# A Strassen-Winograd quad that accumulates two of its seven products in banks of two others

## The chip, the cores and the metric

One core of one Trainium2 chip runs the kernel. The metric is the device time of one execution in microseconds (us); lower is better. TensorE multiplies into PSUM, which has 8 banks of 128x512 fp32 values in this program's use. VectorE (DVE), ScalarE (ACT) and GpSimd (POOL) work on the rest, SP issues the loads.

## The reference

A decoder block on x (1024 tokens by 1024), fp32 in and out:

```
h  = rms_norm(x)
u  = h @ w_in            # recurrent x and gate, q, k, v, two branch gates
y1 = rg_lru(conv4(xr)) * gelu(gr)                  # 16 blocks of 64 channels
y2 = dilated_window_attention(rope(q), rope(k), v) # 3 groups of 4 heads, 128 wide
x1 = x + rms_norm((y1 @ w_lp * sigmoid(gl) + y2 @ w_ap * sigmoid(ga)) @ w_out)
out = x1 + rms_norm((silu(h2 @ w_fg) * (h2 @ w_fu)) @ w_dn),   h2 = rms_norm(x1)
```

D_FF is 2816. The norms have gains. The result is compared at fp32 accuracy, so each fp32 product is made of three matmuls in a faster format: each operand is split into a high part and a rest.

## The kernel before

`split` (L98, L99) makes the two parts of an operand: a copy on ScalarE (names that end in hi or h) and a subtraction on VectorE (lo or l). `mm3` (L133 to L135) issues the three matmuls high by high, rest by high, high by rest for each 128 rows of the contraction.

Most projections are done as 50 objects `Quad`: 28 in phase 1 (four for gr, four for xr, twelve for q and k, eight for the gates gl and ga) and 22 for the FFN (w_fg and w_fu in turn). A quad computes four 128x512 outputs, written (n, u), from two raw 128x1024 weights r0 and r1, with Winograd's form of Strassen's algorithm: seven products P1 to P7 of twelve 128x512 matmuls each, so 84 matmuls a quad. POOL makes the sums of weights sa and sb from r0 and r1 (L267 to L270). Three weight units of a quad go through `split`: r0 for P1 and P2, sa for P6 and P7, sb for P5 and P3; the upper half of r1, for P4, has buffers of its own (w4h, w4l). The pool of the units, tags whi and wlo, has three buffers for each, which go round in the order r0, sa, sb, next r0. The raw weights (tag wraw) have two.

The products run in the order P1, P2, P6, P5, P3, P7, P4, each in its own bank. ScalarE copies P1 out as p1 (L294, `keep`). VectorE adds:

```
out(0,0) = P2 + p1      u2 = P6 + p1      w = P5 + u2      out(0,1) = P3 + w
out(1,1) = P7 + w       v  = P7 + u2      out(1,0) = P4 + v
```

`plus` (L309) makes u2, w and v; the outputs go through `out`, which is L720 in phase 1 (with a function on ScalarE, L722, where there is one, then a DMA), `gate` (L1232 and Silu, L1233) and `up` (L1238, and a product on POOL, L1239) in the FFN. `run_quads` is the loop; after each product `tick` counts, and at fixed counts it emits pieces of other work between the products: the LRU with its convolution (L768 to L800, products `pgt` with operands xch and xcl), and the rotation of q and k (`rotate`, L811 to L816, operands rq, rcs, rsn by DMA).

Phase 1 starts with a stage of its own (0 to 50 us): x arrives, transposed parts are split (`put`, L425 and L426), the squares of the rows give the rates of the norm (`rates`, L439 to L451: square root on ScalarE, five small steps on VectorE, the diagonal dg, and a matmul prb that spreads them), `normed` (L457) scales x, `v0_mm` (L463) makes the first v and `v0_out` (L479) copies it out. The first two quads of phase 1 (PRE1) get their first products ahead of the loop, while the rotary tables are made. At the FFN the list ORDER sets the work ahead of the loop: t is the transposition of a token tile, p the loading of a quad's r0, h a quad's P1 and P2, x the sums of operand columns (splits L562, L563 and differences on POOL, L566).

The order of the instructions on each engine is set by a scheduler from the order in which the program emits them; `tc.issue_after` puts an instruction behind a named one. Loads keep the order of the program on SP.

## Time and profile before

| | |
|---|---|
| median of 3 runs | 1753.15 us (1753.12 to 1754.28) |
| the profiled execution | 1749.78 us |
| its span, first to last instruction | 1748.0 us |
| busy: TensorE, VectorE, ScalarE, GpSimd | 96%, 64%, 42%, 40% |
| mean granted TensorE clock | 0.978 |
| chain that ended last: TensorE, VectorE, DMA | 77%, 8%, 5% |

The profile is of one execution. Busy time is time with an instruction at work; the granted clock is 1.00 at 2.4 GHz and 0.50 at 1.2 GHz. The waits name, for each idle stretch of an engine, the instruction that ended it. Times within the span count from its first instruction.

### The profile page before, as it was taken

The numbers are of one execution on the slowest core, as the hardware profiler recorded it, in microseconds if no ns is written. First come the engines' busy times: TensorE is split into PE (matmuls) and PEld (weight loads), VectorE is DVE, ScalarE is ACT, GpSimd is POOL, SyncE is SP. The second block draws the span as 40 slices with busy tenths as digits, with TensorE's granted clock in tenths as the row PEclk, the third lists the DMA queues.
The fourth block names the chain that finished last, engine by engine and source line by source line (L and its number), as shares of the span: only waits on it lengthen the run. The fifth ranks groups of instructions, "written<-read, shape, count | busy, mean of one in ns | idle before, by whom it ended". The sixth has DMA issues, their size and how long they took to land.

```text
span 1748.0 us, 21093 instructions
## 1 busy us (share of the span) xinstructions
PE 1676.7 (96%) x7748; PEld 1376.2 (79%) x7748; DVE 1113.9 (64%) x1585; ACT 727.5 (42%) x1130; POOL 698.0 (40%) x650
## 2 busy tenths in 40 slices
PE   8999999999999988989999999799999999999996
PEld 6897888787877876878888887678888888788885
DVE  6966676778788665563433577755545555649658
ACT  6423367554555522464451345422222222344343
POOL 2003354554445434214334204576556566400103
PEclk9899999999999999999999999899999999999998
DMA  8233433333333455584618742133222222475353
GB/s 319 73 133 113 148 133 124 135 137 129 127 133 133 139 166 179 197 330 155 229 50 304 269 162 84 49 115 133 102 103 91 103 91 103 150 261 198 109 186 121
DMA packets 95919, 262.70 MB, mean 150 GB/s; under 512 B 13768, under 2 KB 22120, under 8 KB 94408
## 3 DMA queue, kind: packets, MB, share of 16 engines
q1 hardware_dynamic: 70352, 182.49, 30.7%
q0 software_dynamic: 20352, 76.21, 11.5%
q10 hardware_dynamic: 5112, 2.66, 0.5%
q8 instruction: 61, 1.00, 0.2%
q14 instruction: 42, 0.34, 0.1%
HBM read 180.86 MB, written 80.35 MB: 149 GB/s over the span
## 4 chain that ended last, share of the span: by engine, by line
PE 77%; DVE 8%; DMA 5%; issue 4%; POOL 3%; ACT 2%; SPq 1%; ACTq 0%; DVEq 0%; POOLq 0%
PE pq L135 14%; PE pq L134 14%; PE pq L133 14%; PE pd L1334 4%; PE pd L1335 4%; PE pd L1333 4%; DMA rsn<-rtd 3%; PE py L135 2%; PE py L134 2%; PE py L133 2%; PE pv L463 2%; PE po L1017 2%; PE pv L133 1%; PE pv L135 1%; PE pv L134 1%
## 5 line engine op out<-in xcount | busy, mean ns | idle before, releaser
L135 PE MATMUL pq<-hth,wlo 128*128 128x512 f32 x448 | 179.7, 401 | 9.8 <-DVE wlo L99 9.8
L133 PE MATMUL pq<-hth,whi 128*128 128x512 f32 x448 | 179.6, 401 | 2.8 <-ACT whi L98 2.8
L134 PE MATMUL pq<-htl,whi 128*128 128x512 f32 x448 | 180.7, 403 | 0.0
L267 POOL TENSOR_TENSOR sb<-wraw 128x512 f32<-128x512 f32 x50 | 71.6, 1432 | 173.1 <-DMA wraw<-in_w_fg 92.3
L98 ACT ACTIVATE whi<-sa 128x1024 fp32r<-128x1024 f32 x50 | 53.0, 1059 | 201.5 <-PE pq L134 126.8
L1334 PE MATMUL pd<-fbl,fah 128*128 128x512 f32 x304 | 119.7, 394 | 4.5 <-DVE fbl L99 4.5
L1335 PE MATMUL pd<-fbh,fal 128*128 128x512 f32 x304 | 119.7, 394 | 0.0
L1333 PE MATMUL pd<-fbh,fah 128*128 128x512 f32 x304 | 119.3, 393 | 0.0
L98 ACT ACTIVATE whi<-wraw 128x1024 fp32r<-128x1024 f32 x67 | 70.7, 1055 | 98.2 <-PE pq L134 25.8
L135 PEld LDWEIGHTS pq<-hth,wlo 128*128 128x128 f32 x448 | 86.0, 192 | 32.1 <-DVE wlo L99 11.6
L99 DVE TENSOR_TENSOR wlo<-wraw,whi 128x1024 fp32r<-128x1024 f32 x67 | 91.6, 1367 | 26.4 <-ACT whi L98 23.7
L309 DVE TENSOR_TENSOR uw<-pq,uw 128x512 f32<-128x512 f32 x100 | 68.3, 683 | 60.2 <-PE pq L135 59.5
L133 PEld LDWEIGHTS pq<-hth,whi 128*128 128x128 f32 x448 | 86.0, 192 | 24.7 <-ACT whi L98 3.2
L134 PEld LDWEIGHTS pq<-htl,whi 128*128 128x128 f32 x448 | 85.9, 192 | 20.5
L1407 POOL TENSOR_TENSOR y<-y,gpf 128x512 f32<-128x512 f32 x16 | 25.2, 1602 | 186.9 <-ACT fah L98 109.5
L99 DVE TENSOR_TENSOR wlo<-sa,whi 128x1024 fp32r<-128x1024 f32 x50 | 70.1, 1401 | 28.6 <-ACT whi L98 28.6
L1239 POOL TENSOR_TENSOR fo<-fo,ut 128x512 f32<-128x512 f32 x44 | 60.6, 1381 | 67.1 <-DVE ut L1238 67.1
L720 DVE TENSOR_TENSOR fb<-pq,uw 128x512 f32<-128x512 f32 x84 | 67.8, 807 | 29.4 <-PE pq L135 29.0
L99 DVE TENSOR_TENSOR fal<-ar,fah 128x1024 fp32r<-128x1024 f32 (+1 forms) x41 | 50.5, 1231 | 51.5 <-ACT fah L98 51.4
L98 ACT ACTIVATE fah<-ar 128x1024 fp32r<-128x1024 f32 (+1 forms) x41 | 40.8, 995 | 100.9 <-PE pd L1334 79.5
L133 PE MATMUL pq<-t1h,whi 128*128 128x512 f32 x200 | 79.6, 398 | 0.9 <-ACT whi L98 0.9
L134 PE MATMUL pq<-t1l,whi 128*128 128x512 f32 x200 | 79.4, 397 | 0.0
(542 smaller groups left out, 4948.0 us busy)
## 6 DMA issues: line engine op xcount, KB each, us to landing
ar<-fd SPq DMA_DIRECT2D x35, 512.0 KB
qkd<-fb POOLq DMA_DIRECT2D x24, 512.0 KB, 3.6
qk<-qkd SPq DMA_DIRECT2D x24, 512.0 KB
wraw<-in_w_fg SPq DMA_DIRECT2D x24, 512.0 KB
wraw<-in_w_fu SPq DMA_DIRECT2D x24, 512.0 KB
fd<-fo POOLq DMA_DIRECT2D x11, 1024.0 KB, 4.3
wd<-in_w_dn SPq DMA_DIRECT2D x21, 512.0 KB
fd<-fs POOLq DMA_DIRECT2D x11, 768.0 KB, 5.6
```

What stands on the lines that cost most here:

```text
L98: A.activation(hi, src, AF.Copy)
L99: (le or V).tensor_sub(lo, src, f(hi))
L133: T.matmul(o, lh, rh, start=(first and i == 0), stop=False)
L134: T.matmul(o, lh, rl, start=False, stop=False)
L135: T.matmul(o, ll, rh, start=False, stop=(last and i == n - 1))
L267: G.tensor_add(sb[:, lo_], r1[:, lo_], r1[:, hi_])
L309: V.tensor_add(y, bank, x)
L720: V.tensor_add(o, half_in(bank, g), half_in(add, g))
L1239: G.tensor_mul(g, g, ut)
L1333: T.matmul(o, ah[:, ts], bh, start=(i == 0), stop=False)
L1334: T.matmul(o, ah[:, ts], bl, start=False, stop=False)
L1335: T.matmul(o, al[:, ts], bh, start=False, stop=(i == NP - 1))
```

## The change

Each quad now runs P1, P6, P5, P7, P2, P4, P3 in five banks. P2 is accumulated onto P1 in P1's bank (`head2`), after ScalarE has copied p1 out, so that the bank then holds out(0,0) itself; P3 is accumulated onto P5, after ScalarE has copied that out as c1. The additions are

```
u2 = P6 + p1    v = P7 + u2    out(1,1) = c1 + v    out(1,0) = P4 + v    out(0,1) = (P5 + P3) + u2
```

Out(0,0) needs none: in phase 1 and in `gate` ScalarE reads the bank, with the function in the same instruction; in `up` VectorE multiplies the bank with the gate in place. In the ORDER of the FFN, a is P1 with its copy and b is P2. The buffers uw go from three to two, c1 has one. In the start stage some instructions are put behind others: the second `rates` chain, `v0_out`, and the splits `put`.

```diff
-ORDER = [(s[0], int(s[1])) for s in "t6 h1 p2 p3 x5 h0 t7 x6 x4 h2 x7 h3".split()]
+ORDER = [(s[0], int(s[1])) for s in "t6 a1 p2 p3 x5 a0 b1 t7 x6 x4 a2 b0 x7 a3 b2 b3".split()]
...
-        def mm(self, p):
-            bank = ps("pq")
+        def mm(self, p, bank=None):
+
+            first = bank is None
+            bank = bank or ps("pq")
             wh, wl = self.w[p]
             xh, xl = Quad.X[self.NAMES[p]]
             mm3(bank, [(wh[:, 128 * k:128 * k + 128], wl[:, 128 * k:128 * k + 128],
-                        xh[:, k, :], xl[:, k, :]) for k in range(4)])
+                        xh[:, k, :], xl[:, k, :]) for k in range(4)], first, skip_group_check=not first)
...
-        def start_mm(self):
-            self.b = self.mm("P1"), self.mm("P2")
+        def head1(self):
+            self.b = self.mm("P1")
 
         def keep(self):
             self.p1 = Quad.pool.tile([128, 512], F32, name="p1", bufs=Quad.P1B)
-            A.activation(self.p1, self.b[0], AF.Copy)
-
-        def head(self):
-            self.start_mm()
-            self.keep()
+            A.activation(self.p1, self.b, AF.Copy)
+
+        def head2(self):
+            self.mm("P2", self.b)
+            self.whole = True
 
         def first(self):
-            if self.start:
-                self.start()
-            self.out(0, 0, self.b[1], self.p1)
-
-        def body(self):
-
-            def plus(bank, x):
-                y = Quad.up.tile([128, 512], F32, name="uw", bufs=3)
-                V.tensor_add(y, bank, x)
-                return y
-
-            u2 = plus(self.mm("P6"), self.p1)
-            yield
-            w = plus(self.mm("P5"), u2)
-            yield
-            self.out(0, 1, self.mm("P3"), w)
-            yield
-            bank = self.mm("P7")
-            self.out(1, 1, bank, w)
-            v = plus(bank, u2)
-            yield
-            self.out(1, 0, self.mm("P4"), v)
-            if self.done:
-                self.done()
-            yield
+            self.out(0, 0, self.b, None)
 
     def run_quads(quads, pre, tick=None):
+        def plus(bank, x):
+            y = Quad.up.tile([128, 512], F32, name="uw", bufs=2)
+            V.tensor_add(y, bank, x)
+            return y
+
+        step = tick or (lambda: None)
         quads[0].prep()
-        for j in range(pre):
-            quads[j].first()
+        for q in quads[:pre]:
+            if q.whole:
+                q.start()
+                q.first()
         for j, q in enumerate(quads):
             if j + 1 < len(quads):
                 quads[j + 1].prep()
-            for _ in q.body():
-                if tick:
-                    tick()
-            if pre <= j + 1 < len(quads):
-                quads[j + 1].head()
-                if tick:
-                    tick()
-                quads[j + 1].first()
-                if tick:
-                    tick()
+            if j >= pre:
+                q.head1()
+                q.keep()
+                step()
+            if not q.whole:
+                q.start()
+            u2 = plus(q.mm("P6"), q.p1)
+            step()
+            c = q.mm("P5")
+            c1 = Quad.up.tile([128, 512], F32, name="c1", bufs=1)
+            A.activation(c1, c, AF.Copy)
+            step()
+            v = plus(q.mm("P7"), u2)
+            q.out(1, 1, c1, v)
+            step()
+            if not q.whole:
+                q.head2()
+                q.first()
+                step()
+            q.out(1, 0, q.mm("P4"), v)
+            step()
+            q.out(0, 1, q.mm("P3", c), u2)
+            if q.done:
+                q.done()
+            step()
...
-            V.tensor_scalar(dg[:, t], ident, e[:, t:t + 1], None, op0=OP.mult)
+            last_dve[0] = V.tensor_scalar(dg[:, t], ident, e[:, t:t + 1], None, op0=OP.mult)
...
-            put(0, j)
-            w0_split(j)
+            with tc.issue_after(last_dve[0].ins):
+                put(0, j)
+                w0_split(j)
...
-    v0_out(bk0, 0, r0)
+    with tc.issue_after(last_act[0].ins):
+        v0_out(bk0, 0, r0)
     with tc.issue_after(last_rb[0].ins):
         v0_mm(bk1, 1, 1)
     v0_mm(bk1, 1, 2)
     v0_mm(bk1, 1, 3)
-    for j in range(4):
-        normed(1, j, rb)
-    for j in range(4):
-        put(0, j)
+    with tc.issue_after(last_dve[0].ins):
+        for j in range(4):
+            normed(1, j, rb)
+        for j in range(4):
+            put(0, j)
...
-            V.tensor_add(o, half_in(bank, g), half_in(add, g))
-            if fn is not None:
-                A.activation(o, o, fn)
+            if add is None:
+                A.activation(o, half_in(bank, g), fn or AF.Copy)
+            else:
+                V.tensor_add(o, half_in(bank, g), half_in(add, g))
+                if fn is not None:
+                    A.activation(o, o, fn)
...
-        q1[j].start_mm()
+        q1[j].head1()
...
-            V.tensor_add(g, bank, add)
-            A.activation(g, g, AF.Silu)
+            if add is not None:
+                V.tensor_add(g, bank, add)
+            A.activation(g, bank if add is None else g, AF.Silu)
 
         def up(n, u, bank, add):
             g = FO[i][:, 2 * n + u, :]
-            ut = op.tile([128, 512], F32, name="ut", bufs=UT)
-            V.tensor_add(ut, bank, add)
-            G.tensor_mul(g, g, ut)
+            if add is None:
+                V.tensor_mul(g, bank, g)
+            else:
+                ut = op.tile([128, 512], F32, name="ut", bufs=UT)
+                V.tensor_add(ut, bank, add)
+                G.tensor_mul(g, g, ut)
...
+    def head(j):
+        quads[j].head1()
+        quads[j].keep()
+
     for step, j in ORDER:
-        {"p": pre, "h": lambda q: quads[q].head(), "t": e_turn, "x": x_cols}[step](j)
+        {"p": pre, "a": head, "b": lambda q: quads[q].head2(), "t": e_turn, "x": x_cols}[step](j)
```

What moves, in three places.

VectorE in the start stage, from the end of the first four `normed` blocks on. Before:

```order
L426 TENSOR_TENSOR htl_122<-x,hth_120 128x2x512
L441 RECIPROCAL rr_379<-rs_377 128x4
L426 TENSOR_TENSOR htl_122<-x,hth_120 128x2x512
L443 SCALAR_TENSOR_TENSOR re_381<-ss_172,rr_379 128x4
L426 TENSOR_TENSOR htl_123<-x,hth_121 128x2x512
L444 SCALAR_TENSOR_TENSOR re_381<-re_381,rr_379 128x4
L426 TENSOR_TENSOR htl_123<-x,hth_121 128x2x512
L445 SCALAR_TENSOR_TENSOR re_381<-re_381,rr_379 128x4
L99 TENSOR_TENSOR wlo<-wraw,whi 128x1024
L446 TENSOR_SCALAR rr_379<-re_381 128x4
L449 TENSOR_SCALAR dg<-cst,re_381 128x128 x4
L457 SCALAR_TENSOR_TENSOR x<-x,gneg,prb 128x512 x8
```

Now:

```order
L459 SCALAR_TENSOR_TENSOR x<-x,gneg,prb 128x512 x6
L443 RECIPROCAL rr_379<-rs_377 128x4
L445 SCALAR_TENSOR_TENSOR re_381<-ss_172,rr_379 128x4
L446 SCALAR_TENSOR_TENSOR re_381<-re_381,rr_379 128x4
L447 SCALAR_TENSOR_TENSOR re_381<-re_381,rr_379 128x4
L448 TENSOR_SCALAR rr_379<-re_381 128x4
L451 TENSOR_SCALAR dg<-cst,re_381 128x128 x4
L428 TENSOR_TENSOR htl_122<-x,hth_120 128x2x512
L459 SCALAR_TENSOR_TENSOR x<-x,gneg,prb 128x512 x8
L428 TENSOR_TENSOR htl_122<-x,hth_120 128x2x512
L428 TENSOR_TENSOR htl_123<-x,hth_121 128x2x512 x2
L99 TENSOR_TENSOR wlo<-wraw,whi 128x1024 x2
```

The steps of the second `rates` chain (rr, re, dg), which alternated with splits (htl, wlo), follow each other; the splits come behind the chain.

TensorE at the hand-over, from the last matmul of the heads on. Tiles pq are the banks: 1463 is P2 of quad 1, 1546 and 1580 are P6 and P5 of quad 0. Before:

```order
L135 MATMUL pq_1463<-hth1_121,wlo_1447 128x512
L133 MATMUL pq_1546<-hth0_120,whi_1505 128x512 [waits PE_49,Activation_49]
L134 MATMUL pq_1546<-htl0_122,whi_1505 128x512
L133 MATMUL pq_1580<-t1h1_499,whi_1509 128x512 [waits PE_49,Activation_49]
L134 MATMUL pq_1580<-t1l1_500,whi_1509 128x512
L135 MATMUL pq_1546<-hth0_120,wlo_1506 128x512 [waits DVE_49]
```

Now, with 1418 and 1437 as P1 of quads 0 and 1, and 1515 as P6 of quad 0:

```order
L135 MATMUL pq_1437<-hth0_120,wlo_1434 128x512
L133 MATMUL pq_1418<-hth1_121,whi_1414 128x512 [waits Activation_49]
L134 MATMUL pq_1418<-htl1_123,whi_1414 128x512
L135 MATMUL pq_1418<-hth1_121,wlo_1415 128x512
L133 MATMUL pq_1418<-hth1_121,whi_1414 128x512
L133 MATMUL pq_1515<-hth0_120,whi_1479 128x512 [waits PE_49,Activation_49]
L134 MATMUL pq_1515<-htl0_122,whi_1479 128x512
L134 MATMUL pq_1418<-htl1_123,whi_1414 128x512
L135 MATMUL pq_1515<-hth0_120,wlo_1480 128x512 [waits DVE_49]
```

The P2 of quad 0 (L133 with hth1 into 1418) follows the two P1 and waits for ScalarE. Four of its matmuls stand ahead of P6, a fifth behind the first two of P6; the other seven, and the twelve of quad 1's P2, come after the matmul that waits for wlo.

VectorE in the FFN, one quad of the gate with the splits of the next quad's weights among its additions. Before (uw is u2, w and v, fo the outputs):

```order
L1232 TENSOR_TENSOR fo_10508<-pq_10493,p1_10506 128x512
L99 TENSOR_TENSOR wlo_10522<-wraw_10511,whi_10521 128x1024
L309 TENSOR_TENSOR uw_10550<-pq_10537,p1_10506 128x512
L309 TENSOR_TENSOR uw_10565<-pq_10552,uw_10550 128x512
L1232 TENSOR_TENSOR fo_10508<-pq_10567,uw_10565 128x512
L99 TENSOR_TENSOR wlo_10526<-sa_10515,whi_10525 128x1024
L1232 TENSOR_TENSOR fo_10508<-pq_10582,uw_10565 128x512
L309 TENSOR_TENSOR uw_10597<-pq_10582,uw_10550 128x512
L99 TENSOR_TENSOR wlo_10530<-sb_10516,whi_10529 128x1024
L99 TENSOR_TENSOR w4l_10534<-wraw_10513,w4h_10533 128x512
L1232 TENSOR_TENSOR fo_10508<-pq_10599,uw_10597 128x512
```

Now:

```order
L309 TENSOR_TENSOR uw_9890<-pq_9877,p1_9874 128x512
L309 TENSOR_TENSOR uw_9920<-pq_9907,uw_9890 128x512
L1241 TENSOR_TENSOR fo_9876<-c1_9905,uw_9920 128x512
L99 TENSOR_TENSOR wlo_9846<-wraw_9835,whi_9845 128x1024
L99 TENSOR_TENSOR wlo_9850<-sa_9839,whi_9849 128x1024
L99 TENSOR_TENSOR w4l_9858<-wraw_9837,w4h_9857 128x512
L1241 TENSOR_TENSOR fo_9876<-pq_9937,uw_9920 128x512
L1241 TENSOR_TENSOR fo_9876<-pq_9892,uw_9890 128x512
L99 TENSOR_TENSOR wlo_9854<-sb_9840,whi_9853 128x1024
```

Of the seven additions five are left. The split of r0 stood before u2 and comes after out(1,1); the split of sb comes last, after the addition of P3.

## Rows read from the trace of the kernel before

**Rows 1.** Stretches of the span (from:to in us). Columns: length, then busy us and instructions (x) of TensorE's matmuls, of its weight loads, of VectorE, ScalarE and GpSimd, then the granted TensorE clock (1.00 is full speed), the busy share of the DMA engines, GB/s.

```profile
0.00:50.00 50.00, 38.45 (x144) 28.64 (x145) 32.87 (x54) 26.25 (x37) 12.34 (x14) 0.92 0.80 300
...
150.00:165.00 15.00, 11.31 (x42) 8.44 (x41) 6.17 (x8) 6.68 (x9) 9.01 (x10) 0.90 0.33 106
...
350.00:400.00 50.00, 50.00 (x217) 40.38 (x216) 39.02 (x48) 27.52 (x33) 27.22 (x23) 1.00 0.39 140
...
420.00:450.00 30.00, 26.38 (x102) 20.60 (x101) 23.97 (x24) 12.13 (x15) 9.39 (x9) 0.89 0.27 97
...
500.00:550.00 50.00, 49.73 (x212) 39.54 (x212) 45.18 (x50) 25.54 (x32) 22.09 (x20) 1.00 0.34 119
...
650.00:700.00 50.00, 45.06 (x174) 35.44 (x174) 29.09 (x39) 13.43 (x20) 21.22 (x21) 0.90 0.54 182
...
1100.00:1120.00 20.00, 11.19 (x32) 7.61 (x31) 17.33 (x19) 7.96 (x11) 11.21 (x9) 0.66 0.15 52
...
1130.00:1500.00 370.00, 368.81 (x1610) 301.78 (x1609) 200.09 (x215) 104.66 (x134) 233.76 (x178) 1.00 0.29 107
```

**Rows 2.** TensorE's waits over the whole span, the four longest kinds and one more that the prediction counts: the waiting line <- the engine and line waited for: us in total, times, longest.

```profile
PE pq L135 <- DVE wlo L99: 11.4, 6, 4.7
PE pq L133 <- ACT whi L98: 10.0, 4, 5.7
PE prb L451 <- DVE dg L449: 7.0, 1, 7.0
PE pgt L133 <- ACT xch L98: 3.9, 3, 2.2
PE pgt L134 <- DVE xcl L99: 3.3, 5, 1.4
```

**Rows 3.** Groups of instructions over the whole span: VectorE's additions from a bank in the Quads. Behind the bar: busy us, mean ns of one, then idle time before and what ended it.

```profile
L309 DVE TENSOR_TENSOR uw<-pq,uw 128x512 f32<-128x512 f32 x100 | 68.3, 683 | 60.2 <-PE pq L135 59.5
L720 DVE TENSOR_TENSOR fb<-pq,uw 128x512 f32<-128x512 f32 x84 | 67.8, 807 | 29.4 <-PE pq L135 29.0
```

**Rows 4.** Timeline of TensorE in the first 50 us: start, us, line, output <- inputs; in brackets the idle time before and its releaser.

```profile
12.18 2.29 PE L463 MATMUL pv<-wlo,hth 128*128 128x512 f32 x8 [2.09 <-DVE wlo L420]
46.74 2.04 PE L451 MATMUL prb<-dg,ones 128*128 128x512 f32 x2 [6.95 <-DVE dg L449]
```

**Rows 5.** Timeline of VectorE, the chain of L441 to L449 in its two runs: the first and the last row of each.

```profile
22.10 0.17 DVE L441 RECIPROCAL rr<-rs 128x4 f32<-128x4 f32 x1
...
22.97 0.87 DVE L449 TENSOR_SCALAR dg<-cst,re 128x128 f32<-128x128 f32 x4
...
40.84 0.17 DVE L441 RECIPROCAL rr<-rs 128x4 f32<-128x4 f32 x1
...
45.73 0.86 DVE L449 TENSOR_SCALAR dg<-cst,re 128x128 f32<-128x128 f32 x4
```

**Rows 6.** Timeline of ScalarE before the second run of that chain: a split of an operand and the square root (L439).

```profile
38.60 1.06 ACT L425 ACTIVATE hth<-x 128x1024 fp32r<-128x1024 f32 x1
39.55 0.29 ACT L439 ACTIVATE rs<-ss,epsc 128x4 f32<-128x4 f32 x1
```

**Rows 7.** Timeline of TensorE at the hand-over to the Quads: the 25th and the 48th matmul of P1 and P2, and the first ones after them.

```profile
151.65 0.40 PE L133 MATMUL pq<-hth,whi 128*128 128x512 f32 x1
...
157.02 0.40 PE L135 MATMUL pq<-hth,wlo 128*128 128x512 f32 x1
...
160.16 0.50 PE L133 MATMUL pq<-hth,whi 128*128 128x512 f32 x1 [2.75 <-ACT whi L98]
...
161.84 0.77 PE L133 MATMUL pq<-t1h,whi 128*128 128x512 f32 x1 [0.94 <-ACT whi L98]
```

**Rows 8.** Timeline of ScalarE there: the two p1 copies (one row, x2) and the split of the first sa.

```profile
156.61 1.09 ACT L294 ACTIVATE p<-pq 128x512 f32<-128x512 f32 x2 [5.10 <-DMA rtd<-rot]
159.05 1.06 ACT L98 ACTIVATE whi<-sa 128x1024 fp32r<-128x1024 f32 x1 [0.84 <-POOL sa L268]
```

**Rows 9.** The three multiply-adds (L770) of the convolution of one channel block, for two blocks: min/median/max ns, first and last start us.

```profile
L770 DVE SCALAR_TENSOR_TENSOR xc<-xr__3408,vec,xc x3: 744/745/751, 402.3 to 404.3; 128x512 f32<-128x512 f32 x3
L770 DVE SCALAR_TENSOR_TENSOR xc<-xr__3603,vec,xc x3: 752/3208/4284, 425.6 to 433.2; 128x512 f32<-128x512 f32 x3
```

**Rows 10.** Timeline of VectorE in the rotary zone: the last split of a quad's weights (w4l), the second rotation's first product (rm), the split of sa behind it, the next w4l.

```profile
651.93 0.68 DVE L99 TENSOR_TENSOR w4l<-wraw,w4h 128x512 fp32r<-128x512 f32 x1
...
670.41 0.69 DVE L811 TENSOR_TENSOR rm<-rq,rsn 128x512 f32<-128x512 f32 x1 [2.00 <-DMA rsn<-rtd]
...
673.29 1.21 DVE L99 TENSOR_TENSOR wlo<-sa,whi 128x1024 fp32r<-128x1024 f32 x1
...
677.96 0.68 DVE L99 TENSOR_TENSOR w4l<-wraw,w4h 128x512 fp32r<-128x512 f32 x1
```

**Rows 11.** Timeline of VectorE before the FFN's Quads: the same split of one operand part, at two times.

```profile
1087.00 0.68 DVE L563 TENSOR_TENSOR t1l<-h2f,t1h 128x512 fp32r<-128x512 f32 x1
...
1094.67 1.79 DVE L563 TENSOR_TENSOR t1l<-h2f,t1h 128x512 fp32r<-128x512 f32 x1
```

**Rows 12.** Timeline of ScalarE in a quad of the FFN's steady part: the split of sb and the p1 copy.

```profile
1283.02 1.06 ACT L98 ACTIVATE whi<-sb 128x1024 fp32r<-128x1024 f32 x1 [1.64 <-PE pq L134]
...
1288.72 0.60 ACT L294 ACTIVATE p<-pq 128x512 f32<-128x512 f32 x1 [4.64 <-PE pq L135]
```

**Rows 13.** Timeline of VectorE there: the second half of that split of sb.

```profile
1284.74 2.00 DVE L99 TENSOR_TENSOR wlo<-sb,whi 128x1024 fp32r<-128x1024 f32 x1
```

More of the change, by code (lines that the diff above doesn't have):

```diff
@@ L128, in h_tiles, with mm3 @@
         return ts, [ts[k // 4][:, k % 4, :] for k in range(KT)]
-    def mm3(o, terms, first=True, last=True):
+    def mm3(o, terms, first=True, last=True, **kw):
         n = len(terms)
         for i, (lh, ll, rh, rl) in enumerate(terms):
-            T.matmul(o, lh, rh, start=(first and i == 0), stop=False)
-            T.matmul(o, lh, rl, start=False, stop=False)
-            T.matmul(o, ll, rh, start=False, stop=(last and i == n - 1))
+            T.matmul(o, lh, rh, start=(first and i == 0), stop=False, **kw)
+            T.matmul(o, lh, rl, start=False, stop=False, **kw)
+            T.matmul(o, ll, rh, start=False, stop=(last and i == n - 1), **kw)
     def gain_bc(ap, name, eng=None, mk=None):
@@ L237, in block @@
         w = None
+        whole = False
         def __init__(self, src, out, start=None, done=None):
-            self.src, self.out, self.start, self.done = src, out, start, done
+            self.src, self.out, self.start, self.done = src, out, start or (lambda: None), done
         def unit(self, src, names):
```

## Prediction

> **What bounds the kernel now.** I read the stretches of the span first, then TensorE's waits, then the rows around each wait. In the stretches [rows 1] the reader is to see that TensorE is full for most of the span: 217 matmuls in the 50 us from 350, 1610 in the 370 us of the FFN's gate and up. That is 0.230 us for each, at a granted clock of 1.00, and no engine behind it can make it shorter. What the change can win or lose lies in the stretches that are not full: the start (38.45 of 50 us busy, clock 0.92), the hand-over to the quads at 150 to 165 (42 matmuls where 65 fit), 420 to 450 (clock 0.89), 650 to 700 (174 matmuls, clock 0.90) and 1100 to 1120 (32 matmuls, clock 0.66). The waits [rows 2] say on whom: the splits of weights (wlo 11.4, whi 10.0 us), dg once for 7.0 us, and the operands xch and xcl of the LRU's gates for 7.2 us together. VectorE is busy 39 to 45 of 50 us in phase 1, so it is second there, but TensorE waits for it only in places.
>
> The sum is made on the profiled execution, 1749.78 us, of which 1748.0 are the span. The median of the runs, 1753.15, is 3.37 above it; I add that at the end.
>
> **1. Two additions a quad less on VectorE.** Out(0,0) leaves its bank by ScalarE, and the sum w falls away: 0.683 + 0.807 = 1.49 us a quad less in phase 1 [rows 3]. ScalarE gets a copy c1 and, in quads without a function, one of out(0,0): 0.6 us each, the price of the p1 copy [rows 8, 12]. ScalarE is busy for under 28 of those 50 us [rows 1]; the copies hide beside the products, and without that cover they would cost 0.6 us of TensorE each. Where TensorE is full, 1.49 us of VectorE are worth nothing.
>
> **2. Start (0 to 50).** TensorE waits 6.95 us for dg [rows 4]. The chain from rr to dg took 1.74 us the first time (22.10 to 23.84) and 5.75 the second (40.84 to 46.59), because splits of 1.2 us stand between its links [rows 5]. ScalarE's square root was ready at 39.84 [rows 6], so rr also stood 1.0 us behind a split. In the new order the chain is in one piece: 4.0 + 1.0 = **5.0 us** less. Against it, the splits on ScalarE now stand ahead of the square root (0 to 2 us later). For it, the two wlo splits go ahead of htl, which takes away up to the 2.09 us of the wait at 12.18 [rows 4], if what follows moves along; and a shorter idle stretch leaves less time at 1.2 GHz (0 to 2 us; 0.92 over 50 us is 8 us at the lower level, part of it idle anyway). I take **-6**, with ends -3 and -9.
>
> **3. Hand-over to the quads (150 to 165).** Before, the P1 and P2 of both early quads, 48 matmuls, ran up to 157.02, the 25th of them at 151.65 [rows 7]: 0.2335 us each. Then TensorE waited for the split of sa, whose sum POOL finishes at 159 [rows 8]. That time does not change. Now only the two P1, 24 matmuls, can run; P2 goes into P1's bank and waits for the p1 copy, which ScalarE can start only at 156.61, after the rotary table's DMA, and ends at 157.2 [rows 8]. Four matmuls of P2 run in the hole, and 20 are left for after 160.16, where they are in the way: 20 x 0.2335 = **+4.7**. What is queued behind that waiting matmul is all of quad 0. The longer idle stretch may cost some time at the lower clock (here 0.90 over 15 us, [rows 1]): ends +3 and +8.
>
> **4. Phase 1 with the LRU (165 to 600).** The waits for xch and xcl, 7.2 us, and the lower clock in 420 to 450 (0.11 x 30 = 3.3 us) are all that can be won: -10.5. The largest has its cause in one row: the three multiply-adds of a convolution that take 0.745 us alone took 3.21 and 4.28 there, with POOL's four sums of weights running beside them [rows 9]. Fewer additions make VectorE less late; they don't keep the two apart. Against this stands the room of the weight buffers, three of them in rotation. In matmuls between the last use of a buffer and the next unit's first: before 62 to 68 (r0), 38 (sa), 62 to 68 (sb); after, with P2 fifth and P3 seventh, 26, 50 and 26. 26 are 6.0 us. A split pair needs 1.06 + 1.2 us alone [rows 8, 10], and more behind a blocked VectorE. Five quads that are 2.5 us late would cost +12. I take a third of the gain, -4, and +3 for late splits: **-1**, ends -10.5 and +12.
> By the Trainium skill (SBUF — State Buffer, Who interferes with whom) a VectorE instruction with two inputs in SBUF and a GpSimd instruction that reads SBUF shut each other out. The trace agrees: 0.745 against 4.28 us [rows 9], and 0.68 against 1.79 us for the t1 splits of the FFN [rows 11]. By that rule out(1,1), now c1 + v, both in SBUF, would take up to 1.79 us beside POOL; the saving would shrink from 1.49 to 0.4 us a quad, and I would put this term at +1.5 and the median at 1750.4.
>
> **5. Rotation (600 to 720).** From one w4l to the next took 26.0 us [rows 10] against 84 x 0.230 = 19.4 for a quad. After w4l the queue of SP loads two raw weights and then the rotary operands; the second rm ran 18.5 us after w4l, and the split of sa 2.9 us behind that, while TensorE waited. Two additions less per turn are worth 1.4 us, over four turns -5.6. But the split of r0, which stood ahead of the rotary wait, now stands behind it and is due first: I give half back. **-3**, ends -8 and +6.
>
> **6. FFN.** Heads (1080 to 1120): the same splits and POOL differences set the end; T7's transposes come after 24 instead of 48 matmuls and idle time moves forward. **0**, ends -4 and +5. Gate and up: TensorE idles 1.2 us in 370 [rows 1], so nothing can be won. The split of sb took from 1283.02 to 1286.74, 3.7 us with two additions in between [rows 12, 13]; with one more addition and one more copy ahead, 5.0, under the 6.0 of the 26 matmuls. **0**, end +6, if POOL blocks one split more per quad. Down: the order of the last sums moves by up to four POOL operations, read some 30 us later: 0.
>
> **Sum.** -6 + 4.7 - 1 - 3 + 0 = -5.3: 1744.5 in the profiled execution, **1748** as a median.
>
> **Rivals.** *A, late weight buffers (slower).* The 26 matmuls are the mechanism; it decides from the point where release, ScalarE's queue, whi, VectorE's queue and wlo together pass 6.0 us. For it: quads near such a block of VectorE [rows 9], and rotary waits ahead of r0's split. Against: 5.0 us in the FFN, worked out above. Five late quads at 2.5 us in place of my +3 (+9), two rotary turns with r0 late by 3 us (+6), no gain in the rotation (+3) and in the LRU (+4): -5.3 + 22 = +16.7, **1770**; half of all that gives 1759. Chance 0.17.
> *B, VectorE's relief is worth all.* The LRU waits vanish with their clock (-10.5 instead of -1): **1738**. For it: VectorE's 45.18 of 50 us at 500 to 550 falls by 3.8. Against: POOL's part in the longest wait [rows 9]. Chance 0.14.
> *C, the won waits only move.* The start gives 3, since ScalarE's square root is later, the rotation nothing: -3 + 4.7 - 1 = +0.7, **1754**. For it: the order on ScalarE. Chance 0.23.
> *D, the second use of a bank waits in every quad.* P2 waits for p1 three products after P1, 36 matmuls or 8.3 us; the copy takes 0.60. It decides if ScalarE stands 7 us behind. The copies idle before they start (4.64 us at 1288.72, [rows 12]), so only the hand-over shows it. If half of 50 quads lost 0.8 us, +20: **1768**. Chance 0.04.
> The Trainium skill (Perfetto Trace Analysis, Matmuls) says that independent groups should rotate through banks so that emptying one overlaps the next; a bank that is taken up again speaks against the change. Here the row at 156.61 agrees once, in term 3, and the row at 1288.72 does not.
>
> **How the numbers follow.** Forecast 0.42; A 0.17, B 0.14, C 0.23, D 0.04. Its own range is 1742 to 1755. Two in ten may be left out: D, the upper half of A and the far ends of B. **Range 1735 to 1764.** 0.2%, 3.5 us, is about what a measurement here can tell. Faster by more: two thirds of the forecast, B, a little of C: 0.45. Within: a third of the forecast, two thirds of C: 0.28. Slower: A, D, the rest: 0.27.
>
> **What would show it.** Start: dg within 2 us of rr, prb at 40 to 43 instead of 46.74. Hand-over: TensorE idle from about 5 us before the p1 copy, then 20 matmuls of P2 after 160. FFN: 220 matmuls in 50 us still. Wrong: a wait of P1 or P5 for wlo in every quad (A), prb still near 46 (C), or idle time of TensorE in front of P2 for the copy in later quads (D).

## The result, and the profile after

The changed kernel takes 1768.33 us (median of 5 runs, 1767.49 to 1770.72), the kernel before 1754.08 beside it: a ratio of 1.0077, interval 1.0056 to 1.0098, some 14 us **slower**. The forecast was 1748, the range ended at 1764. The profiled execution took 1767.49 us, of which 1765.5 are the span.

The stretches of the changed kernel that answer to [rows 1], and 600 to 650 beside them, in the same columns:

```profile
0.00:50.00 50.00, 44.38 (x179) 34.57 (x180) 36.46 (x60) 27.43 (x38) 12.88 (x14) 1.00 0.74 279
...
150.00:165.00 15.00, 11.40 (x31) 7.96 (x32) 4.12 (x4) 3.72 (x5) 6.98 (x6) 0.66 0.24 81
...
420.00:450.00 30.00, 30.00 (x131) 24.18 (x130) 23.27 (x31) 16.52 (x21) 11.12 (x11) 1.00 0.41 143
600.00:650.00 50.00, 41.69 (x160) 32.78 (x159) 24.96 (x33) 13.77 (x20) 20.54 (x21) 0.90 0.53 174
650.00:700.00 50.00, 41.05 (x162) 32.36 (x161) 23.74 (x33) 12.30 (x18) 20.13 (x21) 0.91 0.51 172
...
1130.00:1500.00 370.00, 366.73 (x1584) 299.27 (x1584) 188.07 (x187) 114.06 (x151) 214.48 (x164) 0.99 0.29 103
```

The start and 420 to 450 are better, as the sum had it. The rotary zone (600 to 720) is worse: 162 matmuls from 650 where [rows 1] have 174, and 160 from 600, where the kernel before has 191 at a higher granted clock:

```profile
600.00:650.00 50.00, 45.10 (x191) 35.79 (x190) 25.58 (x36) 12.18 (x17) 21.09 (x21) 0.97 0.57 179
```

TensorE's longest waits over the whole span, which answer to [rows 2] (fbl, 4.3 us, left out):

```profile
PE pq L135 <- DVE wlo L99: 19.4, 5, 6.1
PE psc L909 <- DMA qk<-qkd: 10.7, 2, 10.0
PE pT L1216 <- DVE xnw L195: 9.5, 2, 8.6
PE pq L133 <- ACT p L297: 6.6, 3, 5.4
PE pq L133 <- ACT whi L98: 5.0, 3, 3.2
...
PE pgt L133 <- ACT xch L98: 3.1, 2, 2.6
PE prb L453 <- DVE dg L451: 3.0, 1, 3.0
```

Splits (wlo) cost 19.4 us where they cost 11.4, and dg fell from 7.0 to 3.0. The attention's qk grew from 6.6 us to 10.7. It was the fourth longest kind before, but [rows 2] go without it, and without the fifth (fbl, 4.5), though they are said to show the four longest:

```profile
PE psc L901 <- DMA qk<-qkd: 6.6, 2, 5.5
```

**Where the time went.** The table compares traces by landmarks: the first or last matmul of a kind, against the same one in the profiled execution of before (1749.78). A quad ends with the last matmul of P4; where P4 runs sixth, the 12 matmuls of P3 behind it are added (2.76 us in phase 1, 2.72 in the FFN). Each number is what the stretch up to the landmark lost (+) or won, in us. The other columns are experiments told below.

| up to | changed | start only (e1) | order alone (e11) | changed, no rotation (e15) | start, no rotation (e16) | best (e10) |
|---|---|---|---|---|---|---|
| first P1, 146.03 before | -4.5 | -3.1 | -2.1 | -3.7 | -2.9 | -2.0 |
| end of quad 0, 176.74 | +3.4 | +1.2 | -0.1 | +2.9 | +0.7 | +0.4 |
| end of quad 20, 598.39 | -3.7 | -2.8 | +1.3 | -3.4 | +0.3 | +0.4 |
| end of quad 25, 711.80 | **+10.5** | +0.8 | +4.9 | -15.6 | -15.6 | -4.9 |
| first py, 766.08 | +4.4 | +0.5 | +6.1 | +4.7 | -0.9 | +0.8 |
| end of the attention, 930.72 | +2.1 | +5.0 | +1.5 | +0.5 | +0.8 | +5.0 |
| last pe, 1070.30 | +0.9 | +1.3 | +0.7 | +0.4 | +0.7 | +1.3 |
| third FFN quad, 1154.59 | +1.9 | 0.0 | +1.3 | +1.8 | +0.8 | +0.6 |
| fourth FFN quad, 1169.96 | +4.6 | 0.0 | +1.6 | +4.7 | 0.0 | -0.1 |
| last FFN quad, 1516.52 | +1.0 | 0.0 | +1.0 | +1.0 | 0.0 | 0.0 |
| last pd, 1734.24 | -3.1 | 0.0 | -3.1 | -3.1 | -1.9 | -1.9 |
| sum | +17.5 | +2.8 | +13.0 | -9.7 | -18.0 | -0.3 |

Each column is one execution, and executions of one kernel differ by several us (e1: 1747.43 to 1757.09), so a column's sum is not its median; what repeats from column to column is what I use. The +10.5 itself does not repeat in size: between the ends of quads 20 and 25, e4 and e5, which keep the order and the rotations, lost 2.2 and 5.1 us, e7 11.7, e11 4.9; e1, with the old order, 0.8. The attention's +5.0, which comes and goes between kernels with the same code there, is not used.

**The rotary zone**, VectorE in the changed kernel:

```profile
597.07 1.23 DVE L99 TENSOR_TENSOR wlo<-sb,whi 128x1024 fp32r<-128x1024 f32 x1
609.27 0.69 DVE L819 TENSOR_TENSOR rm<-rq,rsn 128x512 f32<-128x512 f32 x1 [10.97 <-DMA rsn<-rtd]
...
614.48 0.69 DVE L819 TENSOR_TENSOR rm<-rq,rsn 128x512 f32<-128x512 f32 x1 [0.22 <-DMA rsn<-rtd]
...
618.90 1.22 DVE L99 TENSOR_TENSOR wlo<-wraw,whi 128x1024 fp32r<-128x1024 f32 x1
```

VectorE does nothing for 10.97 us; then come one rotation, the start of a second and two additions, and only then the rest of r0 (wlo<-wraw), which P1 needs. TensorE's row for it:

```profile
620.17 0.80 PE L135 MATMUL pq<-hth,wlo 128*128 128x512 f32 x1 [6.07 <-DVE wlo L99]
```

Three more such waits follow, at 644.88, 669.64 and 696.58, each for the split of r0 behind an rm: 17.3 us with the first. The kernel before had four there too, 9.8 us in all, for the split of sa. The difference is 7.4 us; a clock of 0.90 instead of 0.97 from 600 to 650 makes some 3.5 more (an estimate, 0.07 x 50), so the two come near the 10.5.

In the kernel before the same split stood ahead of the wait:

```profile
605.29 1.23 DVE L99 TENSOR_TENSOR wlo<-wraw,whi 128x1024 fp32r<-128x1024 f32 x1
612.88 0.69 DVE L811 TENSOR_TENSOR rm<-rq,rsn 128x512 f32<-128x512 f32 x1 [6.37 <-DMA rsn<-rtd]
```

### The profile page after: what moved, and what is told of

Same layout as the page of the kernel before. It is cut to its first block, busy times and chain, and to the rows that moved or that the text cites. A ratio compares the mean times of both kernels' runs of the same rounds, so it can differ in the third digit from the quotient of the medians.

```text
span 1765.5 us, 21073 instructions
## 1 busy us (share of the span) xinstructions
PE 1677.5 (95%) x7748; PEld 1375.9 (78%) x7748; DVE 1068.7 (61%) x1496; ACT 760.3 (43%) x1195; POOL 669.5 (38%) x639
## 3 DMA queue, kind: packets, MB, share of 16 engines
q0 software_dynamic: 20352, 76.21, 11.4%
## 4 chain that ended last, share of the span: by engine, by line
PE 49%; DVE 6%; ACT 2%; issue 1%; DMA 1%; POOL 1%; ACTq 0%; DVEq 0%; SPq 0%
PE pq L135 9%; PE pq L133 9%; PE pq L134 9%; PE pd L1350 3%; PE pd L1351 3%; PE pd L1349 3%; PE py L135 2%; PE py L133 2%; PE py L134 2%; PE po L1025 2%; PE pe L135 1%; PE pe L133 1%; PE pe L134 1%; PE ppt L1013 1%; ACT pb L930 1%
## 5 line engine op out<-in xcount | busy, mean ns | idle before, releaser
L135 PE MATMUL pq<-hth,wlo 128*128 128x512 f32 x448 | 181.6, 406 | 17.3 <-DVE wlo L99 17.3
L133 PE MATMUL pq<-hth,whi 128*128 128x512 f32 x448 | 182.2, 407 | 6.9 <-ACT p L297 6.1
L309 DVE TENSOR_TENSOR uw<-pq,uw 128x512 f32<-128x512 f32 x50 | 34.3, 686 | 146.0 <-PE pq L135 146.0
L135 PEld LDWEIGHTS pq<-hth,wlo 128*128 128x128 f32 x448 | 87.1, 194 | 40.7 <-DVE wlo L99 19.9
L133 PEld LDWEIGHTS pq<-hth,whi 128*128 128x128 f32 x448 | 87.3, 195 | 30.0 <-ACT p L297 7.0
L270 POOL TENSOR_TENSOR sa<-wraw 128x512 f32<-128x512 f32 x50 | 70.6, 1413 | 86.1 <-DMA wraw<-in_w_fg 59.2
L268 POOL TENSOR_TENSOR sb<-wraw 128x512 f32<-128x512 f32 x50 | 67.6, 1352 | 70.6 <-DMA wraw<-in_w_g 21.8
L309 DVE TENSOR_TENSOR uw<-pq,p 128x512 f32<-128x512 f32 x50 | 34.4, 688 | 97.4 <-PE pq L135 79.5
L331 ACT ACTIVATE c<-pq 128x512 f32<-128x512 f32 x50 | 29.7, 595 | 144.5 <-PE pq L135 144.5
L1251 POOL TENSOR_TENSOR fo<-fo,ut 128x512 f32<-128x512 f32 x33 | 53.7, 1630 | 98.0 <-DVE ut L1250 88.8
L98 ACT ACTIVATE whi<-sb 128x1024 fp32r<-128x1024 f32 x50 | 52.8, 1057 | 72.9 <-PE pq L134 72.0
L99 DVE TENSOR_TENSOR wlo<-sb,whi 128x1024 fp32r<-128x1024 f32 x50 | 72.2, 1445 | 11.9 <-ACT whi L98 11.9
```

The costliest lines, as they stand in the source:

```text
L98: A.activation(hi, src, AF.Copy)
L99: (le or V).tensor_sub(lo, src, f(hi))
L133: T.matmul(o, lh, rh, start=(first and i == 0), stop=False, **kw)
L135: T.matmul(o, ll, rh, start=False, stop=(last and i == n - 1), **kw)
L268: G.tensor_add(sb[:, lo_], r1[:, lo_], r1[:, hi_])
L270: G.tensor_sub(sa[:, hi_], r0[:, lo_], r1[:, lo_])
```

## The experiments

All stand beside runs of the kernel before on the same chip, whose medians were 1754.53 (e1 to e4), 1753.98 (e5 to e8), 1753.86 (e9 to e12) and 1755.68 (e13 to e16). A ratio is to these.

### The start alone

e1: before.py with the three issue constraints of the diff (on put and w0_split, on v0_out, on normed and put); the quads untouched.

> The kernel before with the change's issue constraints at the start alone (dg in one piece, puts and splits behind it); its quads are the old ones. Theory (the start's part of the change is a gain of its own, about 4.5 us at the first P1, and nothing later takes it back): prb at about 40.6 us instead of 47.7, 4.4 us less in all, about 1749.7. Rival (won waits only move): the gain is swallowed at the hand-over to the quads or later, 1753 to 1755.

1751.83 us, ratio 0.998 (0.9965 to 0.9996). prb runs at 40.7, 7.0 us earlier, and 3.1 are left at the first P1. **Theory, a little smaller**: 3.5 us.

### The hand-over alone

e4, in after.py (shortened, with a comment of mine):

```diff
-        q1[j].head1()
+        q1[j].start_mm()   # P1 and P2 in banks of their own; out(0,0) adds p1
```

> The changed kernel, except that the two early quads of phase 1 run P1 and P2 into banks of their own before the hand-over, as the kernel before did, with the addition of p1 on VectorE for these two. Theory (the hand-over's 20 matmuls of P2 behind the p1 copy cost 4.7 us and nothing else gives them back): 3 to 6 us less, 1762.5 to 1765.5. Rival (the work only moves: the quads that follow wait for their splits instead): within 1.5 us of 1768.3.

1764.59 us (1757.08 to 1769.78), ratio 1.0049 (1.0033 to 1.0065): 0.28% or 4.9 us under the changed kernel's ratio, as the theory had it, though the two intervals overlap (1.0056 to 1.0065). The wait it removes is this one, of TensorE in the changed kernel:

```profile
152.76 0.79 PE L133 MATMUL pq<-hth,whi 128*128 128x512 f32 x1 [5.42 <-ACT p L297]
```

### The order of the products

e11 takes the accumulation out and leaves the order: all additions of the kernel before, banks of their own, the old hand-over (shortened, lines joined):

```diff
-            c1 = ...; A.activation(c1, c, AF.Copy)
+            w = plus(q.mm("P5"), u2)
...
-            v = plus(q.mm("P7"), u2); q.out(1, 1, c1, v)
+            bank = q.mm("P7"); q.out(1, 1, bank, w); v = plus(bank, u2)
-                q.head2(); q.first()
+                q.b2 = q.mm("P2"); q.first()
-            q.out(0, 1, q.mm("P3", c), u2)
+            q.out(0, 1, q.mm("P3"), w)
```

> The change's start and its order of products, P1 P6 P5 P7 P2 P4 P3, but nothing is accumulated: P2 and P3 go into banks of their own and VectorE makes all the additions of the kernel before; the two early quads hand over as before. It differs from the first experiment (1751.8) in the order alone. Theory (the order makes the loss: r0's split must wait for P2, now fifth, and holds the raw buffer and SP's queue): SP waits for wlo over 150 us between 165 and 600, the rotary stretch loses as in the changed kernel, 1761 to 1768. Rival (the accumulation and its copies make it): 1749 to 1754, SP's waits for wlo under 60 us.

1764.22 us, ratio 1.006 (1.0042 to 1.0078). **The order makes the loss**: against e1, which differs in the order alone, 0.8% or 14 us. Against e4, which has the same order with accumulation and copies, 0.1%, within the intervals. SP's waits for wlo (us, times, longest) between 165 and 600, in e1 and in e11:

```profile
SPq L109 <- DVE wlo L99: 27.7, 8, 7.5
```

```profile
SPq L109 <- DVE wlo L99: 212.6, 20, 17.2
```

r0's split waits for the buffers of P2, now fifth, and holds the raw weight that SP's next load needs. e13 and e14 ask which product does it.

e13: as e11, P3 ahead of P4 (P1 P6 P5 P7 P2 P3 P4).

> As the run with the order alone (nothing accumulated, old hand-over, the change's start), but with P3 and P4 exchanged: P1 P6 P5 P7 P2 P3 P4. So only P2 is late (fifth), and P4 is last as in the kernel before. Theory (P2's place holds r0's hi and lo, with them the raw buffer and SP's queue): SP's waits for wlo stay over 150 us between 165 and 600, the rotary stretch loses 4 us or more, 1758 to 1763. Rival (it is P3 as the last product that costs, by the room of the h operands at the start of the attention): 1750 to 1755.

e14: as e11, P2 behind P1 (P1 P2 P6 P5 P7 P4 P3).

> As the run with the order alone, but with P2 behind P1: P1 P2 P6 P5 P7 P4 P3. So only P3 is late (last). Theory: SP's waits for wlo fall under 60 us, the rotary stretch loses under 2 us against the kernel before, the start of the attention 1 to 3 us: 1752 to 1757. Rival (P3's place costs it all): 1760 to 1765.

e13: 1771.18 us, ratio 1.0086 (1.0061 to 1.0112). e14: 1761.29, ratio 1.0034 (1.002 to 1.0047). Both are slower than expected: **"P2 alone" falls**. Against e1, P3 late costs 0.5% by itself, and SP still waits 116.8 us for wlo in e14. P2 late costs 1.1%, though e13 also has P3 one place later than the kernel before, and no less than both late together (e11, 0.8%), so the two do not add up. I take it that each order shortens another slack, which no run shows by itself; e13 lost 7.6 us already between the quads 0 and 20.

e3 and e12 keep the accumulation and move P2 forward (P1 P6 P2 P5 P7 P3 P4; P1 P6 P5 P2 P7 P4 P3).

> The changed kernel with its seven products in the order P1 P6 P2 P5 P7 P3 P4: the same additions and copies, the same accumulation in P1's and P5's banks, but between the last use of a weight buffer and the next unit's first use 50 (r0), 36 (sa) and 50 (sb) matmuls instead of 26, 50 and 26. Theory (short slack of the weight buffers is what loses the time in the quads): the four rotary waits of TensorE fall from 18.9 to under 8 us, the stall of 3.6 us at 1170 goes, 8 to 14 us less: 1754 to 1760. Rival (the accumulation itself, its copies on ScalarE, or the hand-over lose it): 1764 to 1770, with the waits where they were.

> The changed kernel with P2 fourth instead of fifth (P1 P6 P5 P2 P7 P4 P3), accumulated as before in P1's bank, 24 matmuls behind P1 where the run with P2 third had 12. Theory (r0's late release is what costs, and P2 third only failed because it caught up with the p1 copy): no waits of P2 for the copy over 0.5 us outside the hand-over, SP's waits for wlo between 600 and 720 fall from 92 to 40 to 65 us, 1757 to 1764. Rival (any place of P2 behind P6 loses the same): 1766 to 1770; or the copies are late again: over 1772.

e3: 1776.83 us, ratio 1.0129 (1.011 to 1.0147). The waits for wlo fell, as the theory said, and others took their place; TensorE in e3:

```profile
PE pq L133 <- ACT p L297: 14.7, 7, 5.5
...
PE pq L135 <- DVE wlo L99: 8.9, 6, 3.3
PE pgt L133 <- ACT xch L98: 6.5, 5, 1.6
PE pq L133 <- ACT c L335: 4.7, 3, 2.2
```

P2 and P3 catch up with the copies of p1 and c1. Of the 14.7 us, 5.5 are the hand-over's, as in the changed kernel, and four waits in the rotary zone make 8.0; with c1's 4.7, accumulation does wait so close together, which was rival D. It is not all of e3's loss: its trace lost 10.7 us between the quads 0 and 20, where these waits make 3.6. e12: 1769.09, ratio 1.0084 (1.0066 to 1.0102). With P2 two products behind P1 (24 matmuls) the waits for p are those of the changed kernel, but SP's waits for wlo stayed at 87.7 us between 600 and 720: a miss, its rival holds.

### The rotations

e15 and e16: the changed kernel and e1, both without the rotations (in place of `todo.setdefault(ROPE0 + ...)` a `pass`).

> The changed kernel without the six rotations: q and k stay unrotated, and their loads, arithmetic and stores are left out. Theory (10.5 us of the loss belong to VectorE's waits at rm): the ends of quads 20 and 25 lie within 2 us of each other against the kernel before, and it is only 4 to 8 us slower than the same cut from the kernel before with the change's start: 1752 to 1758. Rival (the short slack of the weight buffers costs there without any rotary wait): 11 us or more between the two, 1759 to 1765.

> The kernel before with the change's start, without the six rotations (q and k stay unrotated; loads, arithmetic and stores left out): the counterpart of the run before this one. TensorE's 11 us of rotary waits are gone, some of them given back: 1741 to 1748 by both theories; the difference between the two runs is what tells.

1741.86 us, ratio 0.9927 (0.9908 to 0.9947), and 1731.19, ratio 0.9859 (0.984 to 0.9878). The zone in e15 and in e16:

```profile
600.00:650.00 50.00, 50.00 (x217) 40.29 (x216) 19.72 (x23) 18.40 (x25) 17.51 (x16) 1.00 0.33 119
650.00:700.00 50.00, 50.00 (x216) 40.30 (x215) 19.18 (x24) 18.00 (x25) 17.92 (x18) 1.00 0.36 118
```

```profile
600.00:650.00 50.00, 50.00 (x216) 40.29 (x215) 21.62 (x26) 15.29 (x22) 19.84 (x17) 1.00 0.35 115
650.00:700.00 50.00, 50.00 (x217) 40.29 (x216) 24.17 (x29) 18.18 (x25) 15.49 (x14) 1.00 0.35 115
```

TensorE is full in both, though SP still waits 86.0 us for wlo in e15. So the short slack alone costs nothing there; it costs where the rotations run. That it is VectorE's wait at rm, and not the rotations' own work or transfers, rests on the rows above: no run keeps the rotations and loses that wait. The two differ by 10.7 us in their medians, 0.68% or 12 us by the ratios. That is more than I expected (4 to 8) and near the rival's 11, but not by the rival's mechanism: in the traces it lies after the zone, 5.6 at the start of the attention, 4.7 in the fourth FFN quad.

Four runs tried to take VectorE's wait away by earlier loads. e2: loads four products ahead, on SP. e6: the same on POOL's queue (shortened; the last two lines are e6's, against e2).

```diff
+    def rotate_load(g, u): ...   # t1, t2, cs, sn
-        todo.setdefault(ROPE0 + ROPED * n, []).append((rotate, ...))
+        todo.setdefault(ROPE0 - 4 + ROPED * n, []).append((rotate_load, ...))
+        todo.setdefault(ROPE0 + ROPED * n, []).append((rotate, ...))
-        load(t1, rows[0])            # e6, and so t2, cs, sn
+        G.dma_start(t1, rows[0])
```

> The changed kernel; the four loads of a rotation are issued four products ahead of its arithmetic. Theory (VectorE stands at rm for the sine's DMA, the split of P1's weights is queued behind it, and P1 is due early): TensorE's four waits at 613 to 690, 18.9 us in all, shrink to under 6, and the time falls by 9 to 15 us, to 1753 to 1759. Rival 1 (the weight buffers are short with or without the rotary wait): the waits stay at 12 us or more, 1765 to 1769. Rival 2 (the loads land as late as before, because they stand behind the raw weights on SP's queue): 1766 to 1769, rm still waiting 9 us or more.

> The changed kernel; the four loads of a rotation are issued four products ahead, and by POOL instead of SP, where they stood behind raw weights that wait for w4l. Theory (the loss at 600 to 720 is VectorE standing at rm with P1's split behind it): rm waits under 4 us, TensorE's waits for wlo fall from 19.4 to under 9 us, and the stretch between the ends of quads 20 and 25 gets 7 to 11 us shorter: 1757 to 1762. Rival (POOL's queue is blocked by the loads' own waits for room, so the sums of weights come late): whi or wlo late by as much, 1766 to 1772.

e2: 1765.8 us, ratio 1.0066 (1.0045 to 1.0086), inside the changed kernel's interval. SP in e2 around one rotation, and the rm that waits for it on VectorE:

```profile
593.38 7.84 SPq L109 DMA_DIRECT2D wraw<-in_w_g  x2
...
603.69 0.58 SPq L109 DMA_DIRECT2D rsn<-rtd  x1
```

```profile
614.37 0.69 DVE L825 TENSOR_TENSOR rm<-rq,rsn 128x512 f32<-128x512 f32 x1 [9.37 <-DMA rsn<-rtd]
```

The loads stand behind the raw weights, and the sine needs 10 us from issue to use: rival 2. Since rm waits as before, the theory is not tested. e6: 1780.71, ratio 1.0152 (1.0128 to 1.0177): on POOL's queue the second sine stood behind a quad's sums of weights, which waited for their raw weight; it was issued at 622.01, rm ran at 625.78 after 14.61 us of idle VectorE, and the waits for wlo grew to 29.7 us. A blocked queue, as the rival had it, though blocked by the sums and not by room. The old quads with the same edit (e8):

> The kernel before with the change's start and with the rotary loads four products ahead on POOL's queue; the quads are the old ones. Theory: the start is worth about 4, the rotary waits of the old quads (11.4 us at most) fall by half or more: 1743 to 1748. Rival (the old quads' waits there are for sa's split, which POOL's queue now makes later): 1750 to 1754.

1762.19 us, ratio 1.0042 (1.0024 to 1.0059): the same failure without the new order. e9 and e10 put the loads on SP just ahead of a quad's raw weights (`ROPE0, ROPED` 142, 7, loads four products earlier): e9 in the changed kernel, e10 in e1.

> The changed kernel; the rotations stand seven ticks apart, once a quad, and their loads are issued on SP's queue just ahead of a quad's raw weights instead of behind them, four products before the arithmetic. Theory (SP's queue is held by the raw buffer of r0, which is split late because P2 now runs fifth; the rotary operands land late behind it and VectorE stands at rm with the next split behind): rm waits under 3 us, the stretch between the ends of quads 20 and 25 loses under 3 us instead of 10.5, 1758 to 1762. Rival (the loads' own waits for room in the pool of the LRU hold SP as long): the loss moves to 580 to 640, 1765 to 1772.

> The kernel before with the change's start and with the rotary loads ahead of the raw weights, a quad apart, as in the run before this one; the quads are the old ones. Theory: the start is worth 3 to 4, TensorE's 11 us of rotary waits for wlo fall to under 5: 1743 to 1748. Rival (the rotations come earlier into the last LRU units, whose tiles they share): 1751 to 1756.

e9: 1769.18 us, ratio 1.0086 (1.0068 to 1.0103), half of TensorE's waits moved forward to 595 to 611 (2.9, 2.3 and 2.3 us; SP waited 14.4 us once for the room of POOL's rm), as its rival said. The other half stayed (2.6, 0.8 and 4.5 us at 651, 673 and 697), and the last four rm still waited 9.6 to 11.8 us. e10: **1744.42 us, ratio 0.995 (0.9935 to 0.9966), faster than both kernels**; the zone is 4.9 us shorter than before. Why is open: TensorE's waits for wlo there fell only to 8.4 us (9.9 in e1, under 5 expected) and VectorE's at rm to 32.5 (35.5 in e1); e10 also spaces the rotations a quad apart, and the granted clock is higher than in [rows 1]:

```profile
600.00:650.00 50.00, 43.51 (x185) 34.52 (x185) 30.98 (x41) 12.62 (x18) 25.65 (x25) 0.99 0.59 191
650.00:700.00 50.00, 48.08 (x200) 38.06 (x200) 30.38 (x41) 16.51 (x25) 18.80 (x19) 0.98 0.56 181
```

### The start of the attention

SP in the changed kernel, then in the kernel before:

```profile
746.42 15.93 SPq L109 DMA_DIRECT2D lraw<-ld  x8
762.39 2.78 SPq L109 DMA_DIRECT2D qk<-qkd  x4
```

```profile
740.19 10.59 SPq L109 DMA_DIRECT2D lraw<-ld  x8
750.82 7.23 SPq L109 DMA_DIRECT2D qk<-qkd  x4
```

The eight loads of the LRU's rows (lraw) take room that phase 1's operands held; the second qk stands behind them. P1, P2 and P3 read the h operands. e7: in the last quad of phase 1, P3 ahead of P4.

> The changed kernel, except that the last quad of phase 1 runs P3 before P4. Theory (P3, now last, reads the h operands, in whose room the LRU's rows are loaded next; these loads stand on SP ahead of the second qk, so TensorE's wait for qk grew from 5.9 to 10.4 us): that wait falls to 6 to 8 us, 2 to 4.5 us less, 1764 to 1766.5. Rival (the loads wait for something else): within 1.5 us of 1768.3.

1767.56 us, ratio 1.0073 (1.0052 to 1.0094): the wait for qk fell to 8.4 us and the stretch from 4.4 to 2.9, but the total shows no difference. Over the runs with the rotations the stretch goes by the place of the last product that reads h: seventh, +4.3 to +6.1 (after, e2, e4, e5, e6, e9, e11, e12, e14); sixth, +2.7 to +2.9 (e3, e7, e13); fifth, P3 in the old order, +0.2 to +0.8 (e1, e8, e10).

### The addition c1 + v

e5, in after.py:

```diff
-            c1 = Quad.up.tile(...); A.activation(c1, c, AF.Copy)
...
-            q.out(1, 1, c1, v)
+            q.out(1, 1, c, v)
```

> The changed kernel, except that out(1,1) adds v to P5's product straight from its bank; the c1 copy on ScalarE falls away, so this addition has one operand in SBUF instead of two. Theory (the 3.6 us stall at 1170 and the half clock behind it come from one such addition, which took 6.18 us beside four POOL instructions): no addition of this form over 1 us, the end of the fourth FFN quad 4 to 5 us earlier against its neighbours, 1763 to 1765 in all. Rival (the raw weights are late there anyway): the stall stays, within 1.5 us of 1768.3.

1767.9 us, ratio 1.0075 (1.0047 to 1.0103). Both are half right. The stall at 1170 is gone: the fourth FFN quad wins 0.2 us instead of losing 4.6, and no addition of the line is over 0.69 us. But in phase 1 P3 now waits for VectorE, which must empty P5's bank, where before ScalarE did (TensorE in e5):

```profile
PE pq L133 <- DVE fb L726: 19.2, 8, 7.8
```

The stall, in the changed kernel, on VectorE and on TensorE:

```profile
1165.40 6.18 DVE L1241 TENSOR_TENSOR fo<-c,uw 128x512 f32<-128x512 f32 x1
```

```profile
1173.24 0.80 PE L133 MATMUL pq<-t2h,whi 128*128 128x512 f32 x1 [3.24 <-ACT whi L98]
```

POOL ran from 1165.43 to 1171.01 meanwhile. All additions of that line, with both operands in SBUF and with one in a bank (min/median/max ns):

```profile
L1241 DVE TENSOR_TENSOR fo<-pq,uw x22: 675/680/692, 1142.4 to 1518.2; 128x512 f32<-128x512 f32 x22
L1241 DVE TENSOR_TENSOR fo<-c,uw x11: 691/1868/6179, 1140.0 to 1510.7; 128x512 f32<-128x512 f32 x11
```

The same quad lost time without any c1: 1.6 us in e11, 3.9 in e14, 6.4 in e13, and 2.8 in e8 with the old order. In e14 another instruction with two operands in SBUF met POOL's run, the split of w4l, which takes 0.68 us alone; POOL ran until 1166.47 there, the split until 1167.03:

```profile
1161.44 5.59 DVE L99 TENSOR_TENSOR w4l<-wraw,w4h 128x512 fp32r<-128x512 f32 x1 [1.49 <-issue]
```

In e11 it took 4.95 us. In e13 and e8 no instruction of VectorE took over 3 us there; the cause is not shown. So the addition explains this quad's loss in the changed kernel, and taking c1 away does not by itself keep the quad from it.

## Why the prediction was wrong, point by point

- **1, additions.** Right that two fewer are worth nothing where TensorE is full. In phase 1 they seem to help the new order: between quads 0 and 20 the executions with its additions (changed, e2, e4, e6, e7, e9, e15) won 2.8 to 6.1 us, the one of e11 lost 1.3. Against the old order nothing is shown: e1 won 2.8 there, e16 and e10 lost 0.3 and 0.4.
- **2, start (-6).** Right in its mechanism: -7.1 at prb, -4.5 at the first P1 since 2.6 us came back, with new waits for whi and wlo near 70 (1.8 and 1.2 us). Alone it is worth 3.5 us (e1).
- **3, hand-over (+4.7).** Right in its mechanism: the wait of 5.42 us is there, and it cost 3.4 us in the trace, 4.9 by the ratios of e4.
- **4, LRU (-1).** -3.7. The waits for xch and xcl went from 7.2 to 4.0 us, 420 to 450 is at full clock. The five late quads of rival A didn't come: away from a rotation the 26 matmuls were enough in the changed kernel.
- **5, rotation (-3): the step that failed.** It gave "two additions less per turn", -5.6, half back for r0's split behind the rotary wait. It was +10.5 in this trace, and a loss of 2.2 to 11.7 in the other runs with this order and rotations but unchanged loads. The additions were never on that chain: it runs from w4l over SP's raw loads and the sine's 10 us to rm, and VectorE idles in it. And the split behind rm was not half of a gain but up to 6.1 us of TensorE's time in a turn. I had both numbers, the 18.5 us from w4l to rm [rows 10] and the 6.0 us of the 26 matmuls, and did not subtract. In the changed kernel it was 12.2 us from one split to the next rm (597.07 to 609.27), against that slack of 6.0.
- **6, FFN (0).** Idle time in the heads did move forward (xnw 9.5 us where it was 3.4). +1.9 up to the third quad, +4.6 in the fourth quad, +1.0 spread over the rest, -3.1 in the down projection. The 4.6 is one addition c1 + v beside POOL. By the Trainium skill (SBUF — State Buffer, Who interferes with whom) such an addition and POOL's reads exclude each other; I had put it at up to 1.79 us. The trace agrees with the rule and not with the price: 1.87 us nine times, 6.18 once, with the splits of the next quad behind it. The end of +6 stood for one more split blocked by POOL in each quad; it was one addition in one quad.
- **Not in the sum at all:** the start of the attention, +4.4. I counted the slack of the weight buffers and not of the operands' room, and [rows 2] left out the wait for qk, the row that points there.
- **Rivals.** A had the sign and the size (1770), by half of its mechanism: the rotary turns, not the late quads of the LRU. D did not occur at the distance of 36 matmuls (e11 against e4) nor of 24 (e12), but did at 12 (e3). The rule of the Trainium skill on rotating banks (Perfetto Trace Analysis, Matmuls) is borne out by e3, with 9.2 us of waits for p1 besides the hand-over's 5.5; in the changed kernel the hand-over has 5.4 of 6.6 us.

What stays open: why e13 loses more than e11; of e14's 0.5%, what its trace does not put down to the attention's start (+4.6) and the fourth FFN quad (+3.9); why the down projection won 3.1 us, in e11 too; and how the loss of the order divides between the rotary zone and what follows, since single executions differ by as much.

## What to carry to other kernels

When products change places, count the slack of everything that they hold: weight buffers, raw buffers behind them, the queue behind those, the room of the operands. Compare it with the longest wait that stands ahead of the refill on the same engine, not with the refill's own duration. A gain on an engine is worth nothing on a chain in which that engine idles; and accumulating in a used bank was free here when two or three products stood between (e12, the changed kernel), and not with one (e3).

## What the runs showed of the hardware

One addition of two SBUF operands took 6.18 us beside POOL instructions that followed one another, against 0.69 alone: POOL's run ended at 1171.01, the addition at 1171.58. One split of two SBUF operands took 5.59 us in the same way (e14), against 0.68: POOL's run ended at 1166.47, the split at 1167.03. In both cases the delay lasted until POOL's run ended, not until one of its instructions did. Seven more runs with c1 (e2, e4, e6, e7, e9, e12, e15) have one such addition each, of 5.6 to 6.5 us.
